# Expert inputs scattered to memory by row, and the second layer's expert results stored there

## The chip, the cores and the metric

The kernel runs on one core of one Trainium2 chip, in one launch. The metric is device microseconds of one execution; the median of three runs of the kernel before is 1235.07 us (1232.63 to 1237.51). Engines are called PE (matmuls), DVE, ACT and POOL (elementwise work), SP (it issues most DMAs). A DMA is issued on the queue of an engine; the data are moved by the core's 16 DMA engines.

## What is computed

Two layers, each a sequence mixer (convolution, mLSTM, gated linear recurrence) and a mixture of experts. Layer 1 of the experts (l = 0) runs on 512 tokens, 256 of them context; layer 2 (l = 1, `last` in the code) only on the 256 latent ones. Shapes here: 1024 model columns, 16 experts in 4 groups, two experts per token inside the best group, 512 columns inside an expert.

```python
def hier_moe(h, w_rg, b_rg, w_re, b_re, w_gate, w_up, w_down):
    hf = h.reshape(-1, shp[-1])
    ...
    combine = jnp.sum(jax.nn.one_hot(expert_id, N_EXPERTS) * top_w[..., None], axis=1)
    y = jnp.zeros(hf.shape, jnp.float32)
    for e in range(N_EXPERTS):
        ye = (jax.nn.silu(hf @ w_gate[e]) * (hf @ w_up[e])) @ w_down[e]
        y = y + combine[:, e:e + 1] * ye
    return y.astype(h.dtype).reshape(shp)

for l in range(DEPTH):
    ...
    v_lat = rms_norm(h_lat, norm2_g[l]) * (1 + mod_lat[4]) + mod_lat[3]
    h_lat = h_lat + mod_lat[5] * hier_moe(v_lat, *moe_p)
    if not last:
        ...
        h_ctx = h_ctx + mod_ctx[5] * hier_moe(v_ctx, *moe_p)
```

All is float32. The kernel computes each expert only for the tokens that chose it.

## The kernel before

A stage of the program follows another: mixer 0, the head of layer 1's experts, its 16 experts, mixer 1, head and experts of layer 2, the final norm.

**Head.** The router's choice gives for each token and expert a position in that expert's list (`pos`, `run`, `pm1`); lists have up to 128 places in the code that is concerned here, longer ones are done by `overflow`. The normed tokens vn are turned so that tokens lie on partitions, and split in a high and a low part (`vh`, `vl`) that can be multiplied exactly.

**An expert x** of the loop works in this order, on PE:
- `gu`: gate and up projections of the tokens in `XT` (transposed inputs of a pair of experts), for blocks of 32 or 64 tokens, each under a condition on the expert's count;
- the first turn of `gather` for the next pair `pr`: one-hot matrices P2 (from `onehot`, on DVE) times `vh` and `vl` bring the next pair's tokens, already transposed, into a bank that is copied to `XT`. Four turns make a pair, two in each expert; pair 0 is done in the head by `gather0`;
- `act`: transposes of the activations (8 in all) with silu and product on ACT and DVE;
- the second turn of `gather`;
- the down projection, and what becomes of its result.

**Results.** In layer 1 all experts but the last store their results by list place to Yd in memory (`store`, on ACT's queue); `fetch` gathers them by row for each token (indirect DMAs on POOL, row numbers `rowi`), `take` weights and adds them. In layer 2 every expert is "wide" (`pec`): `down_w`, then `prep` makes scaled one-hots PT, `spread_y` scales and splits, and `to_tokens` brings the result of the expert before to its tokens with matmuls, within the expert after. Yd is zeroed in mixer 0 by 15 stores of SP (line 873).

**Weights.** Each expert has six tiles of 1 MB: gate and up in two halves each, down in two. `ahead` issues them on SP into a ring of slots, 12 in layer 1 and 15 in layer 2, as fast as slots come free; slot names are tags of buffers that are shared with other tiles (`hl`, `uTa`, `uTb`, `B`, the `q4` buffers). `slots` lists them; the seventh load of layer 1, the second expert's first gate half, goes to "hl".

**Order.** PE's order is the one written in the code (a manual schedule); the orders of the other engines are made by a scheduler. DMAs that SP and ACT issue share eight semaphores in rotation (DMAHW0 to 7), so that the n-th waits for the (n−8)-th to have landed; POOL's have eight of their own (DMASW0 to 7).

Of the kernel before, what the change touches and what calls it, by code (L numbers as in the profile page):

```python
# [14 lines left out]
P = 128  # L15
# [11 lines left out]
OVER = 3  # L27
NPE = 1
# [11 lines left out]
def hybrid_kernel(ctx, tc, x, c, cx, c_ctx, w_mod, b_mod, norm1_g, norm2_g, w_in, conv_w, conv_b, conv_ln_g,  # L40
# [15 lines left out]
    Yd = dram.tile([NE - NPE, P, D], F32, name="Yd", tag="Yd")  # L56
    cnt = [0]
# [816 lines left out]


# [210 lines left out]
    def moe(l, hs, fill):  # L1086
# [4 lines left out]
        with tc.tile_pool(name=f"mo{l}", bufs=1, reuse_waits="tile") as mo, \  # L1091
                tc.tile_pool(name=f"op{l}", bufs=1, space=bass.MemoryType.PSUM, reuse_waits="tile") as ops:
            box["ps"], box["nps"] = ops, 4 if last else 6
            NB = {"t2": 3, "t4": 2, "q4": 6, "gr": NT // 2, "sm": 4, "t8": 2 if last else 1, "Y": 2 if last else 3, "Yp": 2}
            yp = "Yp" if last else "q4"

            pec = range(0 if last else NE - NPE, NE)
# [124 lines left out]
            def onehot(pr):  # L1222
                P2 = tmp.tile([P, NT, 256], F32R, "t4" if last else "q4", f"P2_{l}_{pr}")
                for j in range(2):
# [9 lines left out]
            def gather(pr, cp):  # L1234
                XT, P2 = st[pr]
# [37 lines left out]
            V.scalar_tensor_tensor(pm1, pos, 1.0, AA, op0=OP.add, op1=OP.mult)  # L1273
            onehot(0)
# [19 lines left out]
            V.tensor_copy(cnti, cntf)  # L1294

            V.tensor_tensor(m1[4], m1[3], m1[2], op=OP.subtract)
            S.activation(m1[4], m1[4], AF.Exp)
            V.tensor_scalar(m1[5], m1[4], 1.0, None, op0=OP.add)
            V.tensor_tensor(m1[5], m1[5], m1[1], op=OP.mult)
            w1 = m1[6]  # L1300
            V.reciprocal(w1, m1[5])
            w2 = m1[5]
            V.tensor_tensor(w2, w1, m1[4], op=OP.mult)
            spread(A1, oh1)
            spread(A2, oh2)
            A1, A2 = (a.rearrange("p i g j -> p i (g j)") for a in (A1, A2))
            Wt = mt("Wt", [P, NT, NE])
            wtmp = mt("wtmp", [P, NT, NE])
            V.tensor_tensor(Wt, A1, bc(w1, NE), op=OP.mult)
            V.tensor_tensor(wtmp, A2, bc(w2, NE), op=OP.mult)  # L1310
            V.tensor_tensor(Wt, Wt, wtmp, op=OP.add)
            if not last:
                fits = mt("fits", [P, NT, NE])
                V.tensor_scalar(fits, pos, float(P) - 0.5, None, op0=OP.is_lt)
                for x in pec:
                    V.memset(fits[:, :, ORDER[x]:ORDER[x] + 1], 0.0)
                row = mt("row", [P, NT, NE])
                V.tensor_tensor(row, pos, fits, op=OP.mult)
                V.tensor_tensor(row, row, ebase[:, None, :].to_broadcast([P, NT, NE]), op=OP.add)
                rowf = mt("rowf", [P, 2, NT])  # L1320
                rowi = mt("rowi", [P, 2, NT], I32)
                wsel = mt("wsel", [P, 2, NT])
# [6 lines left out]
                V.tensor_copy(rowi, rowf)  # L1329
            show(f"Wt{l}", Wt)  # L1330
# [6 lines left out]
            Z, X1 = [Y2], None  # L1337
            if last:
                X1 = ops.tile([P, 512], F32, name="X1", tag="X1")
                Z.append(ops.tile([P, 512], F32, name="Y3", tag="Y3"))  # L1340
# [19 lines left out]
            def by32(x, b):  # L1360
                return (last and b == 0) if x in pec else (not last and b == 1)
# [32 lines left out]
            def down(b, hT, ps, ws):  # L1394
                w, q = (64, 512) if b == 0 else (32, 256)
                o0 = 256 if b == 2 else 0
                for k in range(4):
                    if b == 0:
                        hk = hT[:, k, :]
                    else:  # L1400
                        hk = hT[:, 2 * (b - 1) + k % 2, 32 * (k // 2):32 * (k // 2) + 32]
# [7 lines left out]
            pend = []  # L1409

            def prep(x):
# [399 lines left out]
```

## Time and profile before

| | |
|---|---|
| median of the runs | 1235.07 us |
| profiled execution | 1238.83 us, span 1237.2 us |
| layer 1's experts on PE | 343.59 to 683.7 |
| layer 2's experts on PE | 947.93 to 1224.81 |
| PE busy | 1102.3 us, 89% |
| DVE, ACT, POOL busy | 634.5, 355.8, 184.4 us |
| DMA | 308.06 MB, mean 249 GB/s |

The span runs from the first to the last instruction of the profiled execution; that execution's own time is 1.6 us longer than its span. The shares are means over stages with different limits. A timeline row gives a start in us from the span's start, a duration, the engine, the line of the kernel, the operation with the tiles that it writes and reads, how many instructions stand in the row, and in brackets the idle time before it with what ended it. A window's row gives the busy time of each engine in a stretch, the clock granted to PE as a share of full speed, the DMA's share and its rate.

### The profile page before, as it was taken

How to read it: one execution, taken by the hardware profiler on the slowest of the kernel's cores; microseconds unless marked ns; L12 is line 12 of the kernel's file. 1: busy time of each engine (PE TensorE's matmuls, PEld its weight loads, DVE VectorE, ACT ScalarE, POOL GpSimd, SP SyncE). 2: the span in 40 equal slices, each digit the busy share in tenths (PEclk: the TensorE clock that was granted, in tenths of full speed). 3: DMA queues.
4: the chain of work that ended last, by engine and by line, in shares of the span. 5: the costliest groups of instructions: out<-in, count | busy, mean ns of one | idle time of the engine just before them, and what ended most of it. 6: DMA issues, size and time to landing. Idle time of an engine off the chain costs nothing. (4 is left out here: it accounts for less than half of the span.)

```text
span 1237.2 us, 21521 instructions
## 1 busy us (share of the span) xinstructions
PE 1102.3 (89%) x8703; PEld 757.8 (61%) x8703; DVE 634.5 (51%) x1411; ACT 355.8 (29%) x696; POOL 184.4 (15%) x143
## 2 busy tenths in 40 slices
PE   6999899999899899999898398989988989999997
PEld 4577688899655454545343166779876645656652
DVE  3879958841721111011101789945946655455553
ACT  3554254432311111111110353734533111111111
POOL 3412213322000000000000633102440000000000
PEclk9989999999999899999999798989898999999999
DMA  9635742575977777866776742345687998979940
GB/s 317 203 103 193 242 137 69 174 269 204 335 315 277 322 270 274 324 250 283 300 319 252 260 137 63 127 136 188 219 307 305 395 385 316 380 294 411 407 163 35
DMA packets 133956, 308.06 MB, mean 249 GB/s; under 512 B 15554, under 2 KB 98798, under 8 KB 113982
## 3 DMA queue, kind: packets, MB, share of 16 engines
q1 hardware_dynamic: 128896, 295.74, 64.6%
q10 hardware_dynamic: 3278, 5.55, 1.2%
q0 software_dynamic: 1648, 4.86, 1.0%
q8 instruction: 100, 1.64, 0.5%
q14 instruction: 34, 0.28, 0.1%
HBM read 296.16 MB, written 12.85 MB: 250 GB/s over the span
## 5 line engine op out<-in xcount | busy, mean ns | idle before, releaser
L1356 PE MATMUL ps<-w,XT 128*64 128x512 f32 x512 | 122.8, 612 | 18.9 <-DMA w<-in_w_up_dram 5.7
L1356 PE MATMUL X<-w,XT 128*32 128x256 f32 (+1 forms) x2016 | 132.0, 393 | 5.2 <-issue 3.1
L1356 PEld LDWEIGHTS X<-w,XT 128*32 128x32 f32 (+1 forms) x2016 | 77.2, 112 | 64.9 <-issue 33.4
L1391 DVE TENSOR_TENSOR hT<-sg,ps 128x256 f32<-128x256 f32 x48 | 19.3, 421 | 188.8 <-ACT sg L1382 188.6
L1356 PEld LDWEIGHTS ps<-w,XT 128*64 128x64 f32 x512 | 43.2, 141 | 94.6 <-issue 63.7
L1242 PE MATMUL ps<-P,vh 128*128 128x256 f32 x336 | 86.1, 293 | 1.7 <-PEq L1636 1.2
L1242 PE MATMUL ps<-P,vl 128*128 128x256 f32 x336 | 82.2, 281 | 0.0
L756 DVE SCALAR_TENSOR_TENSOR acc<-cb,cwh,acc 128x512 f32<-128x512 f32 (+1 forms) x120 | 80.2, 708 | 1.0
L1445 PE MATMUL Y<-w,hT 128*64 128x512 f32 x304 | 73.9, 607 | 1.6 <-DVE hT L1388 0.3
L1242 PEld LDWEIGHTS ps<-P,vh 128*128 128x128 f32 x336 | 63.8, 190 | 11.5 <-PEq L1636 6.2
L1242 PEld LDWEIGHTS ps<-P,vl 128*128 128x128 f32 x336 | 63.8, 190 | 0.5
L1571 POOL DMA_INDIRECT ya<-Yd,rowi x8 | 8.1, 1015 | 358.0 <-issue 358.0
L225 PE MATMUL ps<-w,cS 128*32 128x256 f32 x768 | 49.5, 396 | 9.9 <-DMA w<-in_w_mod_dram 9.6
L1403 PE MATMUL ps<-w,hT 128*64 128x512 f32 x240 | 54.8, 598 | 0.4 <-DVE hT L1391 0.3
L1489 DVE COPY Y<-Y 128x512 f32<-128x512 f32 x15 | 10.4, 692 | 84.8 <-DMA Yd<-Y 41.8
L1379 PE MATMUL ps<-blob,gs 128*128 128x128 f32 x256 | 41.1, 288 | 13.6 <-DVE gs L1368 3.7
L1373 ACT COPY gs<-ps 128x512 f32<-128x512 f32 x15 | 8.8, 586 | 146.0 <-PE ps L1356 107.0
L1445 PEld LDWEIGHTS Y<-w,hT 128*64 128x64 f32 x304 | 24.8, 139 | 34.9 <-issue 32.5
L191 ACT CAST y<-yt 128x512 fp32r<-128x512 f32 x30 | 18.1, 620 | 94.6 <-DVE yt L1461 94.6
L1379 PEld LDWEIGHTS ps<-blob,gs 128*128 128x128 f32 x256 | 27.5, 143 | 28.9 <-issue 12.9
L1246 ACT COPY XT<-ps 128x512 f32<-128x512 f32 x28 | 16.5, 590 | 88.9 <-PE ps L1242 88.5
L1382 ACT ACTIVATE sg<-ps 128x256 f32<-128x256 f32 x64 | 24.2, 388 | 61.9 <-PE ps L1379 61.7
(896 smaller groups left out, 2276.0 us busy)
## 6 DMA issues: line engine op xcount, KB each, us to landing
w<-in_w_down_dram SPq DMA_DIRECT2D x58, 1024.0 KB
w<-in_w_gate_dram SPq DMA_DIRECT2D x49, 1024.0 KB
w<-in_w_mod_dram SPq DMA_DIRECT2D x48, 1024.0 KB
w<-in_w_up_dram SPq DMA_DIRECT2D x48, 1024.0 KB
w<-in_w_in_dram SPq DMA_DIRECT2D x23, 1024.0 KB
w<-in_w_up_dram SPq DMA_DIRECT2D x32, 512.0 KB
w<-in_w_gate_dram SPq DMA_DIRECT2D x30, 512.0 KB
w<-in_w_out_dram SPq DMA_DIRECT2D x8, 1024.0 KB
```

The costliest lines, as they stand in the source:

```text
L191: S.copy(hi, raw)
L225: T.matmul(ps[32 * j:32 * j + 32, hf * 256:hf * 256 + 256], cS[:, k, :], w[:, k, :], start=(k < 4), stop=(k >= 4))
L756: V.scalar_tensor_tensor(acc[:, ch], src, wcol, acc[:, ch], op0=OP.mult, op1=OP.add)
L1242: T.matmul(ps[:, cc, :], v[:, i, k * P:k * P + P], P2[:, i, :], start=(n == 0), stop=(n == 2 * NT - 1))
L1246: S.copy(XT[:, 2 * cp:2 * cp + 2, :], ps)
L1356: T.matmul(ps[w * t:w * t + w, o0:o0 + q], XT[:, k, c0:c0 + w], ws[2 * g + k // 4][k % 4][:, f0:f0 + q], start=(k == 0), stop=(k == KC - 1))
L1379: T.transpose(pt[:, f, :], gs[:, f * P:f * P + P], ident)
L1382: S.activation(sg, pt[:, :, 0:64], AF.Silu)
L1391: V.tensor_tensor(hT, sg, pt[:, :, 64:128], op=OP.mult)
L1403: T.matmul(ps[w * t:w * t + w, o0:o0 + q], hk, ws[4 + k // 2][k % 2][:, q * t:q * t + q], start=(k == 0), stop=(k == 3))
L1445: T.matmul(Z[h][r0:r0 + 64, :], hT[:, k, :], ws[4 + k // 2][k % 2][:, 512 * h:512 * h + 512], start=(k == 0), stop=(k == 3))
L1489: V.tensor_copy(Y, ps)
```

## The change

Four things change.

1. **Inputs of pairs 1 to 7, both layers.** In the head, vn's rows are also copied unsplit (8 and 4 more copies), and indirect DMAs on POOL scatter them to a new tensor Xd in memory, at expert and list place (row numbers `rowx`; 8 scatters of 512 KB in layer 1, 4 in layer 2; in layer 1 the copies lie in the buffers "B" and "hl"). `xload`, on SP, reads a pair's rows back to the single buffer `xg`, which takes "uTb" from the slots (11 and 14 remain): the first 64 places of both experts, and the rest of each under a condition. `gather` is then 4 transposes a turn in place of 16 (layer 1) or 8 (layer 2) one-hot matmuls. Expert 0 has no turns, expert 1 has all four of pair 1, later experts two each. `onehot` remains for pair 0 and the last expert.
2. **Results of layer 2.** Experts 0 to 14 store to Yd as in layer 1, in blocks of 32 for the first 64 places; only the last expert remains wide. `fetch` and `take` are then used in layer 2 as well, at the last expert.
3. **Zeroing.** Xd is zeroed in mixer 0 by 16 stores on SP after Yd's.
4. The head computes `rowx` ahead of the weights of the tokens (`weights`).

```diff
@@ mixer 0 @@
                 for n in range(NE - NPE):
                     nc.sync.dma_start(Yd[n, 64:P, :], z[64 * (n % 2):64 * (n % 2) + 64, :])
+                for n in range(NE):
+                    nc.sync.dma_start(Xd[n], z)
             wvs = [wsplit(w_in[l], 1536 + 256 * hp) for hp in range(2)]
...
-            pec = range(0 if last else NE - NPE, NE)
+            pec = range(NE - NPE, NE)
...
             if last:
-                slots = ["B", "q4", "q4", "q4", "uLa", "uLb", *["r"] * RING, "uTa", "uTb"]
+                slots = ["B", "q4", "q4", "q4", "uLa", "uLb", *["r"] * RING, "uTa"]
             else:
-                slots = ["q4", "q4", *["r"] * 4, "hl", "uTa", "uTb", *["r"] * (RING - 4)]
+                slots = ["q4", "q4", *["r"] * 4, "hl", "uTa", *["r"] * (RING - 4)]
@@ gather @@
                 for cc in range(2):
                     k = 2 * cp + cc
-                    n = 0
-                    for i in range(NT):
-                        for v in (vh, vl):
-                            T.matmul(ps[:, cc, :], v[:, i, k * P:k * P + P], P2[:, i, :], start=(n == 0),
-                                     stop=(n == 2 * NT - 1))
-                            n += 1
+                    for j in range(2):
+                        T.transpose(ps[:, cc, j * P:j * P + P], xg[:, j, k * P:k * P + P], ident)
@@ head @@
+            if last:
+                vn2 = [tmp.tile([P, 2, D], F32, "t8", "vn1")]
...
+            if not last:
+                vn2 = [kt([P, 2, D], name=f"vn{t}", tag=t) for t in ("B", "hl")]
+            vn = [vn2[i // 2][:, i % 2] for i in range(NT)]
...
                     V.tensor_tensor(lo, src, hi.bitcast(F32), op=OP.subtract)
+                    o = vn[i][:, 512 * hf:512 * hf + 512].rearrange("t (k p) -> t k p", k=4)
+                    (S.copy, V.tensor_copy)[hf](o, src)
...
             gather0()
+            Xf = Xd.rearrange("e s d -> (e s) d")
+            for i in range(NT):
+                for cc in range(2):
+                    G.indirect_dma_start(out=Xf, out_offset=bass.IndirectOffsetOnAxis(ap=rowx[:, cc, i:i + 1], axis=0),
+                                         in_=vn[i], in_offset=None, bounds_check=NE * P - 1, oob_is_err=False)
+            xg = kt([P, 2, D], name=f"xg{l}", tag="uTb")
+            G.memset(xg[64:P], 0.0)
+            def xload(pr):
+                if pr < NE // 2:
+                    nc.sync.dma_start(xg[0:64], Xd[2 * pr:2 * pr + 2, 0:64, :].rearrange("e s d -> s e d"))
+                    for j in range(2):
+                        ...
+                        nc.sync.dma_start(xg[64:P, j], Xd[2 * pr + j, 64:P, :], cond=n_x > 64)
@@ expert loop @@
             ahead(0)
+            xload(1)
...
+                turns = ((), ()) if x == 0 else ((0, 1), (2, 3)) if x == 1 else ((2 * (x % 2),), (2 * (x % 2) + 1,))
...
-                if pend:
-                    to_tokens(*pend.pop(), totals())
                 if more:
-                    gather(pr, 2 * (x % 2))
+                    for cp in turns[0]:
+                        gather(pr, cp)
...
                 if more:
-                    gather(pr, 2 * (x % 2) + 1)
-                if last and x + 1 < NE:
-                    prep(x + 1)
+                    for cp in turns[1]:
+                        gather(pr, cp)
+                    if x % 2:
+                        xload(pr + 1)
...
+                elif last:
+                    down(0, hA, Y1, ws)
+                    with tc.If(n_e > 32):
+                        down(1, hA, Y1, ws)
+                    store(x, 0, Y1, n_s)
+                    with tc.If(n_e > 64):
+                        down(None, hB, Y2, ws)
+                    store(x, 1, Y2, n_s)
```

What this does to the order of three queues follows. `w` with a number is a weight tile, `DMAHW`, `DMASW` the DMA semaphores that a row waits for, an engine's name the wait for work of that engine.

SP before, where the experts of layer 1 are first loaded (w67 and w68 are expert 0's down, w69 to w74 all of expert 1, w75 to w80 of expert 2):

```order
L1128 DMA w67_3469<-in_w_down_dram 128x2048 [waits DMAHW7_49,PE_49]
L1128 DMA w68_3471<-in_w_down_dram 128x2048 [waits DMAHW0_49,PE_49]
L1128 DMA w69_3473<-in_w_gate_dram 128x2048
L1128 DMA w70_3475<-in_w_up_dram 128x2048 [waits DVE_49,PE_49]
L1128 DMA w71_3477<-in_w_gate_dram 128x2048 [waits DVE_49,PE_49]
...
L1122 DMA w75_3705<-in_w_gate_dram 128x1024 [waits DMAHW4_49,DVE_49,PE_49]
```

SP after, the same place and what follows, with the read-back of pair 1:

```order
L1134 DMA w67_3531<-in_w_down_dram 128x2048 [waits DMAHW7_49,PE_49]
L1134 DMA w68_3533<-in_w_down_dram 128x2048 [waits DMAHW0_49,PE_49]
L1134 DMA w71_3539<-in_w_gate_dram 128x2048 [waits DMAHW1_49,PE_49]
...
L1134 DMA w79_3757<-in_w_down_dram 128x2048 [waits DMAHW4_49,PE_49]
L1128 DMA w85_3990<-in_w_down_dram 128x1024 [waits DMAHW5_49]
...
L1134 DMA w69_3535<-in_w_gate_dram 128x2048 [waits DMASW2_49,DMASW1_49,DMASW7_49,DMASW0_49,DMAHW7_49,DVE_49,Activation_49]
L1335 DMA xg0_3485<-Xd_64 64x2x1024 [waits DMAHW0_49]
```

The load of w69 has moved from the third place of these to behind expert 2's loads, and waits for four of POOL's DMA semaphores; `xload(1)` stands directly behind it.

POOL before, at the head of layer 1's experts, up to the overflow's branches in expert 3 (branches left out):

```order
L270 TENSOR_TENSOR sq01_2937<-sq01_2937,mhalf_66 128x2 [waits DVE_49]
L270 TENSOR_TENSOR sq00_2995<-sq00_2995,mhalf_66 128x2 [waits DVE_49]
L759 MEMSET wr1_8494 128x256 [waits PE_49]
...
L1497 TENSOR_LOAD cnti0_3417 [waits DVE_49]
L1498 COMPARE_AND_BRANCH
```

POOL after, at the same place:

```order
L762 MEMSET wr1_8327 128x256 [waits PE_49]
L1330 MEMSET xg0_3485 64x2048 [waits DVE_49,PE_49,Pool_49]
L1327 DMA Xd_64<-vnB_3306,rowx0_3382 2048x1024 [waits DMASW3_49,DMAHW6_49,DVE_49,Activation_49]
L1327 DMA Xd_64<-vnB_3306,rowx0_3382 2048x1024 [waits DMASW4_49,DMASW3_49]
...
L1327 DMA Xd_64<-vnhl_3307,rowx0_3382 2048x1024 [waits DMASW1_49,DMASW0_49,Activation_49]
L1327 DMA Xd_64<-vnhl_3307,rowx0_3382 2048x1024 [waits DMASW2_49,DMASW1_49]
```

Eight scatters have come (four of them left out here), each of which waits for a semaphore that the one before it sets; four in layer 2 are chained alike.

SP in mixer 0, before:

```order
L187 DMA w_1066<-in_w_in_dram 128x8x256
L873 DMA Yd<-zero_1197 64x1024 x8
L187 DMA w_1214<-in_w_in_dram 128x8x256
L187 DMA w_1222<-in_w_in_dram 128x8x256
L187 DMA w_1454<-in_w_mod_dram 128x8x256
```

and after:

```order
L190 DMA w_1067<-in_w_in_dram 128x8x256
L876 DMA Yd<-zero_1198 64x1024 x8
L879 DMA Xd<-zero_1198 128x1024 x16
L190 DMA w_1231<-in_w_in_dram 128x8x256
L190 DMA w_1239<-in_w_in_dram 128x8x256
```

The 16 stores of zeros stand between Yd's and the next two weight loads, those of `wvs`.

## Rows read from the trace of the kernel before

**Rows 1.** The page: busy us (share of the span) and instructions of each engine; DMA total.
```profile
PE 1102.3 (89%) x8703; PEld 757.8 (61%) x8703; DVE 634.5 (51%) x1411; ACT 355.8 (29%) x696; POOL 184.4 (15%) x143
...
DMA packets 133956, 308.06 MB, mean 249 GB/s; under 512 B 15554, under 2 KB 98798, under 8 KB 113982
```

**Rows 2.** Timeline of PE, one layer-1 expert: start, us, line, operation, count [idle before].
```profile
382.74 7.09 PE L1356 MATMUL ps<-w,XT 128*64 128x512 f32 x32 [0.65 <-PEq L1674]
389.98 0.35 PE L1242 MATMUL ps<-P,vh 128*128 128x256 f32 x1
...
391.82 0.28 PE L1242 MATMUL ps<-P,vl 128*128 128x256 f32 x1
392.25 1.27 PE L1379 MATMUL ps<-blob,gs 128*128 128x128 f32 x8
...
399.31 1.08 PE L1356 MATMUL ps<-w,XT 128*64 128x512 f32 x4 [0.31 <-PEq L1672]
```

**Rows 3.** Timeline of PE, layer-1 expert 14, and the start of expert 15.
```profile
641.25 7.09 PE L1356 MATMUL ps<-w,XT 128*64 128x512 f32 x32 [0.56 <-PEq L1674]
649.12 1.27 PE L1379 MATMUL ps<-blob,gs 128*128 128x128 f32 x8 [0.78 <-PEq L1649]
...
654.64 1.04 PE L1356 MATMUL ps<-w,XT 128*64 128x512 f32 x2 [0.31 <-PEq L1672]
```

**Rows 4.** Windows: both layers' experts, a full DMA stretch, layer 2's end.
```profile
core 0: us, PE busy (x) PEld busy (x) DVE busy (x) ACT busy (x) POOL busy (x), PEclk, DMA share, GB/s
360.39:683.70 323.31, 297.39 (x2111) 151.53 (x2111) 42.52 (x105) 43.11 (x90) 3.95 (x4) 0.98 0.74 291
948.00:1188.00 240.00, 222.42 (x2323) 142.24 (x2326) 130.32 (x262) 38.71 (x74) 0.65 (x1) 0.99 0.90 359
1110.00:1170.00 60.00, 56.47 (x597) 37.35 (x590) 36.71 (x72) 10.21 (x20) 0.00 (x0) 1.00 1.01 410
1190.00:1225.00 35.00, 33.04 (x259) 15.56 (x257) 12.28 (x25) 2.75 (x6) 0.00 (x0) 0.95 0.01 1
```

**Rows 5.** DMA issues: KB each and median us to landing; window 680:682.5, then whole.
```profile
ya<-Yd,rowi POOLq DMA_INDIRECT x3, 5.8
...
ya<-Yd,rowi POOLq DMA_INDIRECT x8, 8.5
...
rows<-in_conv_w_dram POOLq DMA_DIRECT2D x1, 62.0 KB, 5.0
```

**Rows 6.** Timelines of SP, then DVE, at the head of layer 1's experts.
```profile
325.34 0.42 SPq L1128 DMA_DIRECT2D w<-in_w_gate_dram  x1
...
335.12 3.67 DVE L1287 TENSOR_TENSOR vl<-ps,vh 128x512 fp32r<-128x512 f32 x6
...
343.52 0.16 DVE L1329 CAST rowi<-rowf 128x8 int32<-128x8 f32 x1
```

**Rows 7.** Timelines of SP, ACT and DVE in mixer 0.
```profile
132.44 1.51 SPq L187 DMA_DIRECT2D w<-in_w_in_dram  x2
...
141.28 1.04 ACT L191 CAST w28h<-w 128x1024 fp32r<-128x1024 f32 x1
...
154.31 1.22 DVE L192 TENSOR_TENSOR w28l<-w,w28h 128x1024 fp32r<-128x1024 f32 x1
```

**Rows 8.** Timeline of PE: a layer-2 expert with few tokens, and the last one.
```profile
962.31 3.66 PE L1356 MATMUL X<-w,XT 128*32 128x256 f32 x64 [0.16 <-PEq L1664]
...
972.84 3.65 PE L1445 MATMUL Y<-w,hT 128*64 128x512 f32 x16
976.65 4.73 PE L1356 MATMUL X<-w,XT 128*32 128x256 f32 x82
...
1199.90 7.11 PE L1356 MATMUL X<-w,XT 128*32 128x256 f32 x128
1206.94 2.12 PE L1478 MATMUL ps<-y,PT 128*128 128x512 f32 x8
...
1217.72 7.09 PE L1445 MATMUL Y<-w,hT 128*64 128x512 f32 x32
```

More of the change, by code (lines that the diff above doesn't have):

```diff
@@ L27 @@
 OVER = 3
+NOROW = 65536.0
 NPE = 1
@@ L1222, in onehot @@
             def onehot(pr):
-                P2 = tmp.tile([P, NT, 256], F32R, "t4" if last else "q4", f"P2_{l}_{pr}")
-                for j in range(2):
+                P2 = None
+                js = {0: (0, 1), NE // 2 - 1: (1,)}.get(pr, ())
+                if js:
+                    P2 = tmp.tile([P, NT, 256], F32R, "t4" if last else "q4", f"P2_{l}_{pr}")
+                for j in js:
                     e = ORDER[2 * pr + j]
@@ L1294, in moe, with weights @@
             V.tensor_copy(cnti, cntf)
[L1296 to L1314, printed above, removed]
+            def weights():
+                V.tensor_tensor(m1[4], m1[3], m1[2], op=OP.subtract)
+                S.activation(m1[4], m1[4], AF.Exp)
+                V.tensor_scalar(m1[5], m1[4], 1.0, None, op0=OP.add)
+                V.tensor_tensor(m1[5], m1[5], m1[1], op=OP.mult)
+                w1 = m1[6]
+                V.reciprocal(w1, m1[5])
+                w2 = m1[5]
+                V.tensor_tensor(w2, w1, m1[4], op=OP.mult)
+                V.tensor_tensor(Wt, A1, bc(w1, NE), op=OP.mult)
+                V.tensor_tensor(wtmp, A2, bc(w2, NE), op=OP.mult)
+                V.tensor_tensor(Wt, Wt, wtmp, op=OP.add)
                 for x in pec:
                     V.memset(fits[:, :, ORDER[x]:ORDER[x] + 1], 0.0)
[L1317 to L1322, printed above, removed]
+                V.tensor_tensor(row, row, fits, op=OP.mult)
                 V.tensor_tensor(fits, fits, Wt, op=OP.mult)
@@ L1329, in moe @@
                 V.tensor_copy(rowi, rowf)
+            Wt = mt("Wt", [P, NT, NE])
+            rowi = mt("rowi", [P, 2, NT], I32)
+            wsel = mt("wsel", [P, 2, NT])
+            weights()
             show(f"Wt{l}", Wt)
@@ L1360, in by32 @@
             def by32(x, b):
-                return (last and b == 0) if x in pec else (not last and b == 1)
+                return last and b == 0 if last or x in pec else b == 1
             def evac(x, b, ps):
@@ L1408, in moe @@
             pt_ = {}
-            pend = []
             def prep(x):
@@ L1615, in moe @@
                                          max_val=NTOK)
-                elif not last:
-                    if x == pec[0]:
-                        fetch()
-                    if x == NE - 1:
+                else:
+                    fetch()
+                    if not last:
                         box["w0"] = [wsplit(w_in[1], a) for a in (0, 256)]
-                    Z[1:] = [bank()]
-                    V.memset(Z[1], 0.0)
+                        Z[1:] = [bank()]
+                        V.memset(Z[1], 0.0)
                 pa = X1 or bank()
-                if wide and last:
+                if last:
                     gu(x, 0, pa, ws)
-                    if x == 0:
+                    if wide:
                         prep(x)
@@ L1678, in moe @@
                 if x == OVER:
-                    if last:
-                        to_tokens(*pend.pop(), totals())
-                    else:
-                        gr = gate_rows(l, 5, mo, "gr", (0, 1), NT // 2)
+                    gr = gate_rows(l, 5, mo, "gr", range(NT // 2), NT // 2)
                     overflow()
@@ L1779, in _constants @@
     a[:, C_IOTA:C_IOTA + 128] = t + 1
-    for x in range(NE - NPE):
+    for x in range(NE):
         a[:, C_MISC + ORDER[x]] = 128 * x
```

113 lines of the change are left out of this document (57 added, 56 removed).

## The prediction

> **What bounds the kernel now.** I read the page first. TensorE (PE) is busy 89% of the span and the 16 DMA engines move 249 GB/s on average [rows 1]; such a mean hides stages, so I then read a table of windows. In layer 1's experts (from the second expert's start at 360.39 to 683.70) PE is busy 297.39 of 323.31 us and the DMA moves 291 GB/s; in layer 2's experts (948 to 1188) it moves 359, at a share of 0.90, and where it is full (1110 to 1170, share 1.01) 410, which I take as its ceiling [rows 4]. After 1190 there are no loads left, and PE still works until 1225 [rows 4]: it had fallen behind. So PE sets the end of both stages, with the DMA close behind it in layer 2. The timeline of PE then tells what an expert is made of [rows 2, 3].
>
> **What goes from PE in layer 1.** An expert with up to 64 tokens takes 399.31 − 382.74 = 16.57 us: gate and up 7.09, two turns of 16 gather matmuls, 8 transposes of its activations, down. One turn runs from 389.98 to 391.82 + 0.28, 2.1 us (the rows between are 14 of the same kind) [rows 2]. Seven pairs times four turns make 28 turns, 59 us; E0's two run before 360.39, so 26 turns, 55 us, lie behind it. In their place stand 16 transposes per pair. Eight transposes take 1.27 us [rows 2], so 16 take 2.5, at most 18 us for seven pairs. But the turns also covered waits: expert 14, which gathers nothing, takes 654.64 − 641.25 = 13.39 us and shows an idle 0.78 ahead of its transposes that the others don't [rows 3]. That is 3.2 less than 16.57. With its share of the transposes, partly in those gaps, an expert comes to about 14.0, so 2.5 us less on 13 experts: **−33 us**, not 55 − 18 = −37.
>
> **What the scatters add in layer 1.** In the new order each scatter on POOL waits for the semaphore of the one before it: eight in a chain. And the load of the second expert's first gate half (w69) goes to the slot that now holds half of the scatters' source; it waits for the last of them. Before it was issued at 325.34, before the experts began [rows 6]. Queued behind it on SP are pair 1's read-back and all further loads; PE has nothing to do between expert 0 and expert 1 but wait. The chain starts when the row numbers are there: the nearest row, the cast of rowi, is at 343.52 [rows 6], so about 345. The trace holds no scatter. The nearest row is the gather of the same size by row, 5.8 us from issue to landing with the DMA busy; over all eight of them it is 8.5; the shortest queue of POOL's that the trace shows, for 62 KB, is 5.0 [rows 5]. I take 5.8, since few of the loads are in flight beside this chain: 8 x 5.8 = 46 us, bounds 40 and 68. It ends at 391; w69 lands some 6 us later (one more link of the same kind, behind little else), so expert 1 starts at about 397 instead of 360.39: **+37 us**, from +31 to +59.
> The Trainium skill, DMA: Bandwidth & Descriptors (section Anatomy of one DMA — SWDGE (gpsimd) path), puts such a DMA at about 2.0 us plus its bytes over 436 GB/s. By it an estimate for 512 KB is 3.2 us and for the chain 26, and the sum would be 20 us less. The rows' 5.0 for 62 KB speaks against it in this kernel; no run shows a scatter yet.
>
> **Loads in layer 1.** Of PE's 323.31 us 26 are idle [rows 4]; I take them for waits on weights. From 397 on 78 of the 96 tiles are still to come, 82 MB, and about 11 MB of read-backs, stores and fetches: 93 MB. With 290 us for it that is 320 GB/s, above the 291 of before and below the ceiling of 410 [rows 4]. So it fits, but with one slot fewer (11 for 12) and the single buffer xg, whose read-back waits on SP for the last transposes of the pair before, with the loads queued behind it. I add **+8 us** (0 to 15) to the waits of before. Layer 1 in sum: +37 − 33 + 8 = +12.
>
> **Mixer 0.** 16 zero stores of 512 KB, 8.4 MB, stand on SP ahead of two weight loads issued at 132.44 [rows 7]. At the ceiling of 410 they take 20 us. The loads were cast at 141.28, but the low half of the first was made only at 154.31, behind other work on DVE [rows 7], and the matmuls that use it follow. 141.28 + 20 + 1.04 (the cast) = 162 against 154.31: up to 8 us later, less where the loads had landed well ahead of the cast, more by a few where the zeros don't reach the ceiling. **+6 us** (0 to 12).
>
> **Head.** Each head copies vn too: half the copies on DVE behind vl's, eight and four in all. One vl subtraction of that size is 3.67 / 6 = 0.6 us [rows 6]; the four on DVE in layer 1 are 2.4, half of it ahead of the gather of pair 0. **+1 us** for both layers.
>
> **Layer 2.** PE loses much here. An expert with up to 32 tokens runs from 962.31 to 976.65, 14.3 us [rows 8]. Of that go 2.1 for the spreading of the results of the expert before (2.12 in the last one), two gather turns of half the length (2.1, with 1.2 for the transposes that come), about 1 for the scaled one-hots and half of the 3.65 of down: it falls to about 8.5 us. Its six tiles are 6.3 MB, 15 us at 410. So PE's gain is nearly all lost: the DMA becomes the bound. The weights of 948 to 1188 are 240 us x 359 = 86 MB; the change adds 4 scatters, 7 read-backs, 15 experts' stores and 4 fetches, 11 MB by their sizes. 97 MB at 410 is 237 us: without any idle the last load lands at 1185, with the tenth of idle that the stage has now (24 us) at 1209. In the new order SP also waits for the four scatters (4 x 5.8 = 23 us) before it goes on past pair 1's read-back. Behind the last load, the second half of down, there remain most of the last expert's 24.9 us (1199.90 to 1217.72 + 7.09), less 2.12 for spreading and 5 for gate and up having landed two tiles earlier: 18 [rows 8]. 1209 + 18 = 1227 against 1224.8; with a few us of waits between stores on ACT and loads on SP, which share eight semaphores in rotation, **+4 us**, from −18 (no idle) to +12. What follows, the last adding to tokens and the output, stays.
>
> **Sum.** 12 + 6 + 1 + 4 = +23 us. The profiled execution took 1238.83 us with a span of 1237.2, 3.8 above the median of 1235.07; the difference is put on the median: 1258.
>
> **The rivals.**
> A, the forecast: 1258. Chance 0.56, spread from 1238 to 1280 by the bounds above.
> B, faster: the chain goes at 5.0 a link and the loads keep near 410. Then expert 1 starts 31 us late, the 33 us of gathers go, and half of the 26 us of weight waits goes too, since no one-hot buffer of a pair blocks the shared buffers any more: −15 in layer 1. In layer 2 the idle tenth fills: −18; mixer +2, head +1: −30, **1205**. For it: PE lost 33 and more in both layers and the ceiling leaves room in layer 1. Against: the stage mean has never been near 410 while slots turned over. It decides if the DMA's share is above 0.95 in layer 2 from its start. Chance 0.18.
> C, read-backs stall PE in layer 1: xg is issued in the middle of an odd expert and its first transposes come some 12 us later (down 3.7, gate and up 7.1, the turn). If eight tiles stand ahead of it in the DMA queue, 8.4 MB at 410 is 20 us, so 8 us too late, seven times 56; some 16 of that is in A's waits already: +40, **1298**. For it: one buffer only. Against: the weights ahead of it mostly wait for slots and are issued behind it. Chance 0.13.
> D, nothing to measure: the link of 5.8 holds waiting in full queues. Its bytes at 410 GB/s are 1.3 us, the least a link can be; halfway from there to 5.8 a link is 3.6, the chain 29 and not 46, expert 1 starts 17 us earlier, and layer 2 comes out even: 23 − 17 − 4 = +2, **1237**. For it: the DMA has little to move while the chain runs. Against: 5.0 for 62 KB. The rule of the Trainium skill quoted above (same page and section) gives nearly this. Chance 0.13.
>
> **How the numbers follow.** A measurement of this kernel tells about 0.5% (6 us) from no change. Faster: B and a little of A, 0.20. Same: most of D and A's lower edge, 0.16. Slower: the rest of A, and C, 0.64. The range from 1210 to 1298 leaves out half of B, half of C and the tails.
>
> **What would show it.** The scatters' issues on POOL, 5.8 us apart from about 345; a gap on PE before expert 1 of some 40 us, ended by the load of w69; experts of about 14 us in layer 1 and none of 16.6; in layer 2 a DMA share near 1 while PE waits for weights, and the end of loads only some 18 us ahead of PE's end, where 37 lay. In mixer 0 the first use of the two loads about 6 us late. I am wrong if the gap before expert 1 is under 25 us, if PE waits for xg in every pair, or if the loads of layer 2 end before 1195 less the shift of what came before.

## The result and the profile after

The changed kernel takes 1363.63 us (median, 1360.52 to 1365.68) against 1233.85 for the kernel before, measured with it: a ratio of 1.1045, interval 1.1008 to 1.1081. The forecast was 1258, with a range to 1298: the direction was right, but the time lies outside the range, and the loss, 130 us, is more than five times the 23 forecast. The profiled execution has a span of 1358.6 us, 121.4 longer than the span before. Lines of the changed kernel are a little further down than in the listing above: `gu` is L1402, `gather` L1250, the weight loads L1128 and L1134, the read-back L1335 and L1340.

The page's busy times and its DMA total, to lay beside [rows 1]:

```profile
PE 1034.5 (76%) x8207; PEld 685.4 (50%) x8207; DVE 531.6 (39%) x1181; ACT 369.3 (27%) x719; POOL 211.7 (16%) x165
...
DMA packets 144357, 337.41 MB, mean 248 GB/s; under 512 B 16548, under 2 KB 102352, under 8 KB 124640
```

PE does 68 us less and idles 189 us more; 29 MB more are moved at the same mean rate. The stages, read from PE's timeline (first and last matmul of each, us):

| stage | before | after | difference | forecast |
|---|---|---|---|---|
| mixer 0 and head, to expert 0's gate | 343.6 | 351.9 | +8.3 | +7 |
| layer 1: expert 0's gate to expert 1's gate | 16.8 | 54.3 | +37.5 | +37 |
| layer 1: expert 1's gate to the last down | 323.4 | 350.4 | +27.0 | −25 |
| mixer 1 and head | 264.2 | 265.3 | +1.1 | 0 |
| layer 2's experts | 276.9 | 321.2 | +44.3 | +4 |
| final norm and output | 12.4 | 15.5 | +3.1 | 0 |

Two rows of the table hold nearly all of the error: layer 1 after expert 1's start, 52 us, and layer 2, 40 us. The windows of these two stretches, to lay beside [rows 4], and of the kernel before the whole of layer 2; the last three columns are the granted clock, the DMA's share and its GB/s:

```profile
406.20:756.60 350.40, 279.93 (x1807) 116.82 (x1807) 36.03 (x70) 45.48 (x91) 7.21 (x8) 0.92 0.75 276
1021.90:1343.10 321.20, 205.66 (x2433) 122.41 (x2432) 43.40 (x88) 50.16 (x98) 11.84 (x11) 0.81 0.83 306
...
947.90:1224.80 276.90, 257.24 (x2593) 158.90 (x2592) 143.46 (x287) 41.46 (x80) 0.65 (x1) 0.98 0.79 313
```

In layer 1 the DMA is 0.75 busy and moves 276 GB/s, where it was 0.74 busy and moved 291 before. In layer 2 it is 0.83 busy at 306; over the whole stage it was 0.79 and 313 before (the 0.90 and 359 of [rows 4] leave out the end of the stage, which has no loads). So the DMA is not at its ceiling, and PE, idle for 70 us in layer 1 and 116 in layer 2, isn't busy either: both wait. What for, the views of waits tell (us in total, times, longest; SPq is SP's DMA queue): SP's in layer 1 from expert 1 on, in layer 2, and of the kernel before in layer 1:

```profile
SPq L1134 <- DMA Yd<-Y: 102.1, 10, 15.5
SPq L1128 <- DMA Yd<-Y: 32.0, 5, 15.0
SPq L1340 <- DMA Yd<-Y: 31.2, 2, 16.8
...
SPq L1134 <- DMA Yd<-Y: 73.6, 9, 13.9
...
SPq L1128 <- DMA Yd<-Y: 29.4, 5, 12.3
...
SPq L1128 <- DMA Yd<-Y: 80.8, 5, 18.0
SPq L1122 <- DMA Yd<-Y: 63.0, 5, 17.6
```

A load or read-back on SP waits here for a store of results, Yd<-Y, that ACT has issued: 165 us in layer 1, 103 in layer 2 (where the kernel before had no such stores), 144 in layer 1 before. One such wait in layer 2, with the timelines of ACT, SP and PE and windows of 4 us:

```profile
1214.30 1.77 ACTq L1518 DMA_DIRECT2D Yd<-Y  x3
...
1212.12 0.33 SPq L1134 DMA_DIRECT2D w<-in_w_gate_dram  x1
1226.37 0.33 SPq L1134 DMA_DIRECT2D w<-in_w_up_dram  x1
1226.79 0.66 SPq L1335 DMA_DIRECT2D xg<-Xd  x1
...
1217.08 1.92 PE L1402 MATMUL X<-w,XT 128*32 128x256 f32 x28 [0.61 <-DMA w<-in_w_up_dram]
1234.34 1.08 PE L1250 MATMUL ps<-blob,xg 128*128 128x128 f32 x4 [15.33 <-DMA xg<-Xd]
...
1216.00:1220.00 4.00, 2.40 (x36) 0.91 (x28) 0.00 (x0) 0.59 (x1) 0.00 (x0) 1.00 1.01 409
1220.00:1224.00 4.00, 0.00 (x0) 0.00 (x0) 0.00 (x0) 0.00 (x0) 0.00 (x0) 0.91 0.77 320
1224.00:1228.00 4.00, 0.00 (x0) 0.00 (x0) 0.00 (x0) 0.00 (x0) 0.00 (x0) 0.50 0.32 63
```

ACT stores an expert's results at 1214.30. SP's next load, of w_up, has its place in the rotation of eight semaphores behind that store, and is issued only when it has landed, at 1226.37; the read-back stands behind that. Meanwhile the DMA runs dry (63 GB/s in 1224 to 1228), PE waits 15.33 us for xg, and its granted clock, 0.91 in 1220 to 1224, is 0.50 in the next window, the lower of its two levels, 1.2 GHz; PE has been idle since 1219. Then the next expert begins the same round. PE's longest waits over the whole program are the read-backs and the load behind the chain of scatters:

```profile
PE ps L1250 <- DMA xg<-Xd: 101.2, 16, 15.5
PE ps L1402 <- DMA w<-in_w_gate_dram: 41.4, 3, 37.6
```

The chain of scatters took about the time that was forecast. POOL's, SP's and PE's timelines; then the DMA issues with their median us to landing, in layer 1 for the scatters from "B" and from "hl", and in layer 2:

```profile
351.82 1.13 POOL L1327 DMA_INDIRECT Xd<-vnB,rowx  x1 [6.91 <-DVE XT L1269]
359.84 0.99 POOL L1327 DMA_INDIRECT Xd<-vnB,rowx  x1 [6.88 <-DMA Xd<-vnB,rowx]
...
385.23 0.96 POOL L1327 DMA_INDIRECT Xd<-vnhl,rowx  x1 [6.74 <-issue]
...
396.97 0.97 POOL L1327 DMA_INDIRECT Xd<-vnhl,rowx  x1 [2.61 <-DMA Xd<-vnhl,rowx]
...
400.83 0.33 SPq L1134 DMA_DIRECT2D w<-in_w_gate_dram  x1
...
406.22 9.39 PE L1402 MATMUL ps<-w,XT 128*64 128x512 f32 x32 [37.60 <-DMA w<-in_w_gate_dram]
```

```profile
Xd<-vnB,rowx POOLq DMA_INDIRECT x4, 6.9
...
Xd<-vnhl,rowx POOLq DMA_INDIRECT x4, 3.5
...
Xd<-vn,rowx POOLq DMA_INDIRECT x4, 3.3
```

From the first issue at 351.82 to the last landing at 400.6 are 48.8 us, forecast 46. The first four links run beside weight loads and land after 6.9 us, the last four in a DMA with little else to do after 3.5. By the Trainium skill, DMA: Bandwidth & Descriptors (section Anatomy of one DMA — SWDGE (gpsimd) path), such a DMA takes about 2.0 us plus its bytes over 436 GB/s, an estimate of 3.2 us for 512 KB. The trace agrees with it (medians of 3.3 and 3.5) where few loads are under way and not where they are (6.9).

In mixer 0, SP's and PE's timelines:

```profile
132.19 19.23 SPq L879 DMA_DIRECT2D Xd<-zero  x16
151.52 2.74 SPq L190 DMA_DIRECT2D w<-in_w_in_dram  x2
...
161.30 1.22 PE L520 MATMUL ps<-w28h,uh0a 128*128 128x256 f32 x4 [9.78 <-ACT w28h L194]
```

The zeros hold SP until 151.52, 19 us later than the loads were issued before [rows 7], and PE waits 9.78 us for the cast of what the loads bring.

### The profile page after: what moved, and what is told of

It reads as the page before. It is cut to its first block, busy times and chain, and to the rows that moved or that the text cites. A ratio compares the mean times of both kernels' runs of the same rounds, so it can differ in the third digit from the quotient of the medians.

```text
span 1358.6 us, 20751 instructions
## 1 busy us (share of the span) xinstructions
PE 1034.5 (76%) x8207; PEld 685.4 (50%) x8207; DVE 531.6 (39%) x1181; ACT 369.3 (27%) x719; POOL 211.7 (16%) x165
## 5 line engine op out<-in xcount | busy, mean ns | idle before, releaser
L1402 PE MATMUL ps<-w,XT 128*64 128x512 f32 x512 | 132.1, 629 | 65.6 <-DMA w<-in_w_gate_dram 41.4
L1402 PE MATMUL X<-w,XT 128*32 128x256 f32 (+1 forms) x2016 | 138.9, 401 | 17.4 <-PEq L1700 6.5
L1250 PE MATMUL ps<-blob,xg 128*128 128x128 f32 x224 | 44.8, 332 | 102.4 <-DMA xg<-Xd 101.2
L1402 PEld LDWEIGHTS X<-w,XT 128*32 128x32 f32 (+1 forms) x2016 | 80.2, 114 | 76.2 <-issue 35.4
L1402 PEld LDWEIGHTS ps<-w,XT 128*64 128x64 f32 x512 | 41.3, 143 | 153.1 <-issue 108.4
L1250 PEld LDWEIGHTS ps<-blob,xg 128*128 128x128 f32 x224 | 32.3, 171 | 117.7 <-issue 98.0
L1514 DVE COPY Y<-Y 128x512 f32<-128x512 f32 x30 | 20.7, 691 | 140.4 <-PEq L1700 38.5
L1419 ACT COPY gs<-X 128x512 f32<-128x512 f32 x45 | 26.3, 589 | 175.3 <-PEq L1674 57.4
L1450 PE MATMUL Y<-w,hT 128*32 128x256 f32 (+1 forms) x912 | 63.9, 420 | 7.1 <-DMA w<-in_w_down_dram 4.6
L1425 PE MATMUL ps<-blob,gs 128*128 128x128 f32 x256 | 48.3, 331 | 26.7 <-ACT gs L1419 18.3
L1450 PEld LDWEIGHTS Y<-w,hT 128*32 128x32 f32 (+1 forms) x912 | 29.8, 119 | 38.8 <-issue 18.5
L1254 DVE COPY XT<-ps 128x512 f32<-128x512 f32 x28 | 19.2, 687 | 68.7 <-PE ps L1250 68.6
L1450 PEld LDWEIGHTS ps<-w,hT 128*64 128x64 f32 x240 | 17.0, 148 | 40.0 <-issue 30.1
```

The source lines that it names most:

```text
L1250: T.transpose(ps[:, cc, j * P:j * P + P], xg[:, j, k * P:k * P + P], ident)
L1254: V.tensor_copy(XT[:, 2 * cp:2 * cp + 2, :], ps)
L1402: T.matmul(ps[w * t:w * t + w, o0:o0 + q], XT[:, k, c0:c0 + w], ws[2 * g + k // 4][k % 4][:, f0:f0 + q], start=(k == 0), stop=(k == KC - 1))
L1419: S.copy(o, src)
L1425: T.transpose(pt[:, f, :], gs[:, f * P:f * P + P], ident)
L1450: T.matmul(ps[w * t:w * t + w, o0:o0 + q], hk, ws[4 + k // 2][k % 2][:, q * t:q * t + q], start=(k == 0), stop=(k == 3))
```

## The experiments

**Theories.** *Bytes*: the DMA is the bound, time follows the bytes (the forecast's view of layer 2). *Read-back*: read-backs stand in SP's queue behind loads and stall PE (rival C). *Ring*: the stores of results in the semaphore rotation (this rotation is what is called the ring from here on) keep the loads from running ahead. *Slot*, its rival in the expectations from e5 on: the loads wait for slots that PE frees, and the waits for stores only lie on top. They give different times when one thing is moved at a time.

**e1, results only.** All gathers stay one-hot in both layers; no scatter, no xg, no zeros of Xd. The edit of `gather`; the rest is taken away in the same way.

```diff
-                        T.transpose(ps[:, cc, j * P:j * P + P], xg[:, j, k * P:k * P + P], ident)
+                        for i in range(NT):
+                            for v in (vh, vl):
+                                T.matmul(ps[:, cc, :], v[:, i, k * P:k * P + P], P2[:, i, :], ...)
...
```

> Layer 2's results go through memory as in the changed kernel, but both layers gather by one-hot matmuls as before (no scatter, no read-back, no zeroing of Xd, the slot uTb given back). Read-back theory (the changed kernel loses its time on read-backs that stand in SP's queue and share semaphores with the stores, and on the chain of scatters): both are gone, layer 1 is as before (E1 starts near 360, layer ends near 684), layer 2 is shorter than before by some 10 us because PE does less and only the DMA limits; 1220 to 1232 us. Bytes theory (the DMA is the bound, time follows the bytes): 5 MB more than before in layer 2 is 12 us, so 1240 to 1250. If the stores alone hold up the loads through the shared semaphores: over 1255.

1249.82 us, ratio 1.0136 (1.0099 to 1.0173). Layer 1 is as before (339.9 against 340.2 us), layer 2 takes 283.5 us against 276.9, though PE does far less there (220 us busy against 257). So the stores alone cost more than they save. The time lies where Bytes put it (1240 to 1250); what parts Bytes from Ring is e5.

**e2, read-backs on POOL's queue.**

```diff
-                    nc.sync.dma_start(xg[0:64], Xd[2 * pr:2 * pr + 2, 0:64, :].rearrange("e s d -> s e d"))
+                    nc.gpsimd.dma_start(xg[0:64], Xd[2 * pr:2 * pr + 2, 0:64, :].rearrange("e s d -> s e d"))
...
```

> The changed kernel with the read-backs issued on POOL's queue instead of SP's, same bytes, same single buffer. Read-back theory: the read-back no longer stands behind weight loads nor waits for the landing of the stores of results; PE's waits for xg (about 101 us in the changed kernel, 80 of them in layer 2) fall below 40 and the time to 1290 to 1320. Bytes theory: same bytes, so 1350 to 1365. The chain before expert 1 (a gap of 37.6 us) stays in both.

1359.95 us, ratio 1.102 (1.0967 to 1.1074): no gain. PE's waits:

```profile
PE ps L1402 <- DMA w<-in_w_gate_dram: 47.3, 6, 38.4
PE X L1402 <- DMA w<-in_w_up_dram: 38.8, 21, 4.8
...
PE ps L1250 <- DMA xg<-Xd: 19.6, 3, 17.7
```

The wait for xg falls from 101.2 to 19.6 as expected, and waits for weights take its place. So the read-back theory falls as it was stated: the read-back was only what came last; the loads were late anyway. This time, too, lies where Bytes put it.

**e3, no slot "hl".** Layer 1 has 10 slots, and no load waits for the scatters.

```diff
-                slots = ["q4", "q4", *["r"] * 4, "hl", "uTa", *["r"] * (RING - 4)]
+                slots = ["q4", "q4", *["r"] * 4, "uTa", *["r"] * (RING - 4)]
```

> The changed kernel with the slot hl taken out of layer 1's ring (10 slots instead of 11), so that no weight load waits for the scatters. Chain theory: expert 1's first gate half loads early, its gate and up run right after expert 0, and only its gather turns wait for the chain of eight scatters; the gap of 37.6 us before expert 1 goes, a gap of some 25 to 30 us comes before its first transposes of xg; net gain 8 to 15 us, less what one slot fewer costs: 1345 to 1360. If the gap was not due to that load: the gap stays, 1363 to 1375.

1355.96 us, ratio 1.0984 (1.0943 to 1.1026). PE's timeline:

```profile
371.89 7.09 PE L1402 MATMUL ps<-w,XT 128*64 128x512 f32 x32 [0.31 <-PEq L1707]
...
409.79 0.45 PE L1250 MATMUL ps<-blob,xg 128*128 128x128 f32 x1 [27.23 <-DMA xg<-Xd]
```

Expert 1's gate comes at 371.9 instead of 406.2, its first transposes of xg at 409.8 instead of 419.1; the layer ends no earlier (760.2). The gap was due to that load, but it wasn't what the layer's end hung on.

**e4, scatter in layer 1 only.** Layer 2 gathers by one-hot, as in e1.

> Scatter and read-back in layer 1 only; layer 2 gathers by one-hot and has its results through memory. Read-back theory: layer 1 as in the changed kernel (E1 near 406, end near 757), layer 2 loses its 80 us of waits for xg and takes about 265 to 275 us instead of 321: 1305 to 1320. Bytes theory: only 6 MB go, 15 us: about 1348.

1323.85 us, ratio 1.0705 (1.0668 to 1.0743): between what Read-back and Bytes gave. Layer 2's scatter costs 40 us of the changed kernel, layer 1's 74 (against e1).

**e5, stores on POOL's queue.** The direct test of the ring; the same bytes, the same loads.

```diff
-                    nc.scalar.dma_start(Yd[x, s0:s0 + w, :].rearrange("s (h f) -> h s f", f=q), Y[:, q * c:q * c + q],
+                    nc.gpsimd.dma_start(Yd[x, s0:s0 + w, :].rearrange("s (h f) -> h s f", f=q), Y[:, q * c:q * c + q],
```

> The changed kernel with the stores of results (Yd) issued on POOL's queue instead of ACT's, so that they leave the rotation of eight semaphores that the weight loads go through; same bytes. Ring theory (a weight load waits for the landing of the store issued eight DMAs earlier, which itself waits for an expert's end, so the loads can't run ahead): SP's 268 us of waits for Yd go, 1270 to 1310 us, with the 38 us gap of the scatter chain left. Slot theory (the loads wait for slots that PE frees, the stores' waits only lie on top): 1345 to 1365. Bytes theory: 1355 to 1365.

1278.78 us, ratio 1.0338 (1.0321 to 1.0355), as Ring gave it: 85 us less by the queue of the stores alone, with the same slots. In SP's waits none for results in Yd is left. So neither the bytes nor the slots were the bound for these 85 us. The move also takes the issue of the stores from ACT: PE's waits for ACT's copies (gs) fall from 18.3 to 8.1 us. So some 10 of the 85 may be that, which no run parts from the ring.

**e6, e1 with the stores on POOL.**

> e1 (results of layer 2 through memory, all gathers by one-hot) with the stores on POOL's queue. Ring theory: e1's 275 us of waits of SP for Yd go and with them PE's waits for w_up and w_gate in layer 2; 1200 to 1222, faster than both kernels. Slot theory or bytes theory: as e1, 1243 to 1255.

1192.49 us, ratio 0.9641 (0.9623 to 0.9659): faster than both kernels, and by more than Ring gave.

**e7, the kernel before with the stores on POOL.**

> The kernel before with layer 1's stores on POOL's queue. Ring theory: the ring held up loads there too (SP waited 165 us for Yd), but PE was idle for only 26 us in layer 1, so at most that can go: 1212 to 1228. Slot theory: no change, 1230 to 1238.

1210.31 us, ratio 0.9785 (0.9769 to 0.9802), a little less than Ring gave. Layer 1 from expert 1 on, to lay beside the 323.31 us of [rows 4]:

```profile
359.50:666.70 307.20, 289.92 (x2111) 151.45 (x2111) 46.54 (x110) 47.42 (x94) 27.26 (x54) 0.99 0.83 313
```

The ring was there before; it cost 16 us in layer 1 (324.0 against 340.2) and 8 in mixer 1 (256.6 against 264.2). So storing layer 2's results (e6 against e7) is worth 18 us where the stores don't hold up the loads, and cost 14 (e1) where they do.

**e8, stores and read-backs on POOL, no slot "hl".**

> The changed kernel with stores and read-backs on POOL's queue and without the slot hl: three couplings taken away at once. Ring theory: 1235 to 1275, of which 25 to 30 us are the chain of scatters before the first read-back and 8 us the zeroing. Slot theory: above 1330, since one slot fewer is left.

1259.76 us, ratio 1.018 (1.0161 to 1.0199). Still 67 us behind e6. Windows of e5 and of e6, for layer 1 from expert 1 on and for layer 2:

```profile
407.80:703.40 295.60, 263.07 (x1807) 113.67 (x1807) 38.15 (x73) 45.53 (x91) 26.48 (x51) 0.97 0.93 330
964.20:1260.90 296.70, 199.56 (x2433) 117.44 (x2432) 43.34 (x88) 49.91 (x97) 27.24 (x56) 0.84 0.91 332
...
359.70:666.90 307.20, 290.43 (x2111) 151.47 (x2111) 47.85 (x110) 47.41 (x94) 28.44 (x55) 0.99 0.84 316
923.70:1173.70 250.00, 207.70 (x2545) 124.95 (x2544) 46.45 (x105) 48.89 (x97) 23.22 (x52) 0.95 0.92 367
```

In layer 1 the transposes leave PE with 263 us of work in e5, the gathers with 290 in e6; yet the stretch is only 11.6 us shorter. The DMA is 0.93 busy in e5 and moves 330 GB/s with it, where e6 moves 316 with 0.84. In layer 2, 0.91 busy brings 332 GB/s, in e6 0.92 brings 367. So with read-backs a busy DMA seems to move less; these are means over whole stages, and e13 tests it.

**e9 and e10, the chain hidden, the zeros late.** Pair 1 is gathered by one-hot matmuls too, so that the scatters have until pair 2. In the expectations from here on, Read-back means that reading back costs DMA time. e10 also issues the zeros behind the two loads.

```diff
-            xload(1)
+            xload(2)
...
-                js = {0: (0, 1), NE // 2 - 1: (1,)}.get(pr, ())
+                js = {0: (0, 1), 1: (0, 1), NE // 2 - 1: (1,)}.get(pr, ())
...
-                    if x % 2:
+                    if x % 2 and pr > 1:
```

> e8 (stores and read-backs on POOL, no slot hl) with pair 1 gathered by one-hot matmuls in experts 0 and 1, in both layers, so that the chain of scatters has until pair 2. Chain theory: the gaps before the first transposes of xg in e8 (30.9 us in layer 1, 21.5 in layer 2) go and with them 40 to 50 us: 1208 to 1220. Read-back theory (in e8 the DMA was busy 0.90 to 0.95 at only 340 GB/s, so reading back costs DMA time and the loads used the gaps): 15 to 30 us go, 1230 to 1245.

> e9 with the 16 stores of zeros to Xd issued after the two weight loads that they stood in front of in mixer 0. If the 8 us that the first experts start later in the changed kernel come from these stores: 5 to 8 us less than e9. If from the head's extra copies: 0 to 2 us less.

1250.89 us, ratio 1.0136 (1.0103 to 1.0169), and 1243.8, ratio 1.0067 (1.0047 to 1.0087). Hiding the chain brings 9 us by the medians (5 by the ratios, whose intervals overlap), though PE waited over 50 for it in e8; both theories gave more. That the loads run ahead while PE waits is my reading, without a run for it; e9 also gives PE pair 1's one-hot matmuls back. The zeros' place is worth 7 (expert 0's gate at 347.2 instead of 352.5); 3.6 us of the later start remain, which I put down to the head's copies without a run for it.

**e11 and e12, scatter in one layer only, all of that out of the way.** e11 in layer 1 with the zeros late, e12 in layer 2.

> Scatter in layer 1 only, with pair 1 by one-hot, zeros late, stores and read-backs on POOL, no slot hl; layer 2 gathers by one-hot. To compare with e6 (1192.5), which has no scatter. If taking the gather matmuls off PE pays once chain, stores and zeros are out of the way: layer 1 takes 300 us or less against 324 in e6, 1165 to 1178. Read-back theory: the DMA becomes the bound in layer 1 too, 315 to 330 us, 1185 to 1205.

> Scatter in layer 2 only, with pair 1 by one-hot, stores and read-backs on POOL; layer 1 gathers by one-hot. To compare with e6 (1192.5). Read-back theory: layer 2 is bound by the DMA in e6 already (0.92 busy, 367 GB/s), so PE's gain is worth nothing and the extra 7 MB cost 20 to 40 us beside the 5 to 8 of the zeros: 1215 to 1240. If only the chain hurt there: 1197 to 1205.

1210.65 us, ratio 0.9782 (0.9747 to 0.9817), and 1233.33, ratio 0.9982 (0.9967 to 0.9996). Both are slower than e6 with no scatter, by 18 and 41 us: e11 lies above the range that Read-back gave, e12 in its own. Of the 41 some 8 are the zeros, which stand early in e12 (expert 0's gate at 351.2 against 343.0 in e6); of the 18 some 4 are the later start (347.1). e11 in layer 1, and e12 in layer 2, to lay beside e6's above:

```profile
363.90:681.00 317.10, 265.61 (x1823) 119.90 (x1823) 37.20 (x72) 45.60 (x92) 38.38 (x76) 0.94 0.91 333
...
935.50:1219.80 284.30, 204.83 (x2449) 117.11 (x2448) 43.08 (x90) 49.84 (x97) 32.57 (x74) 0.89 0.91 344
```

In e11 PE's work is 25 us less than in e6, and the stretch is 10 us longer, with the DMA at 0.91 and 333 GB/s. In e12 it is 3 us less and the stretch 34 us longer.

**e13, e14, e17, e18, the pieces of it in layer 2 with PE's work as in e6.** The gathers stay one-hot, and what is moved besides isn't used: the read-backs alone (e13), the scatters alone (e14), the same reads from rows of w_down (e17), and nothing but the slot taken away that xg takes (e18). All read-backs are on POOL's queue. e17's edit, against e13:

```diff
-                    nc.gpsimd.dma_start(xg[0:64], Xd[2 * pr:2 * pr + 2, 0:64, :].rearrange("e s d -> s e d"))
+                    nc.gpsimd.dma_start(xg[0:64], w_down[l, 2 * pr:2 * pr + 2, 0:64, :].rearrange("e s d -> s e d"))
...
```

> e6 with layer 2's seven read-backs of Xd (zeros, never scattered to) done beside the one-hot gathers and not used; one slot fewer, zeros of Xd issued late. To compare with e6 (1192.5). If the read-back is dear by itself: 4.2 MB cost 20 us or more, 1212 to 1225. If it costs only its bytes at 410 GB/s: 10 us or less, 1195 to 1205.

> e6 with layer 2's four scatters (and the extra copies of vn) done beside the one-hot gathers and never read; no zeros. If only the read-back is dear: 2 MB at 410 GB/s, 5 us, 1194 to 1200. If the scatters hold up the loads: above 1205.

> e13 with the seven unused reads taken from rows of w_down instead of Xd, same shapes, same queue, no zeros. If any such reads beside the loads cost that: as e13, 1208 to 1215. If it is the reading of Xd: 1195 to 1203.

> e6 with one slot fewer for layer 2's weights (14 instead of 15), which the read-back buffer takes; nothing else. If the slot is part of e13's 20 us: 1197 or more; otherwise 1190 to 1195, as e6.

1212.55 (ratio 0.982, 0.9797 to 0.9843), 1193.12 (0.9651, 0.9625 to 0.9677), 1212.34 (0.9816, 0.98 to 0.9832) and 1192.25 us (0.9659, 0.9642 to 0.9676). Against e6's 1192.49 the scatters and the slot cost nothing that the runs can tell; reading 4 MB beside the loads costs 20 us, twice what they take at 410 GB/s, from either tensor. e13's windows, 40 us with read-backs and 40 after them, then its DMA queues in each (packets, MB, share; q1 carries SP's loads, q0 what POOL issues):

```profile
966.00:1006.00 40.00, 28.89 (x364) 19.15 (x359) 4.64 (x12) 6.63 (x14) 3.99 (x9) 0.87 1.02 343
1046.00:1086.00 40.00, 34.73 (x364) 19.51 (x358) 7.42 (x19) 7.59 (x17) 2.92 (x6) 0.96 1.02 411
...
q1 hardware_dynamic: 2015, 11.50, 82.3%
q0 software_dynamic: 1008, 2.10, 18.9%
...
q1 hardware_dynamic: 2584, 15.68, 96.0%
```

The DMA is full in both (1.02); with the read-backs it moves 343 GB/s, without them 411. The loads themselves are slowed: 11.50 MB in 82.3% of 40 us are 349 GB/s, 15.68 in 96.0% are 408. POOL's queue is not the reason. In e5 SP issues the read-backs, and a slow stretch of a full DMA follows each of layer 2's last five; two windows of 4 us from one of them, in which PE waits for xg:

```profile
1072.00:1076.00 4.00, 0.00 (x0) 0.00 (x0) 0.00 (x0) 0.00 (x0) 0.00 (x0) 0.50 1.03 226
1076.00:1080.00 4.00, 0.00 (x0) 0.00 (x0) 0.00 (x0) 0.00 (x0) 0.00 (x0) 0.50 1.03 197
```

**e15 and e16, another layout of xg.** The pair's experts lie in the lower and the upper 64 partitions, so that both halves are written. The edit against e12 and e11:

```diff
-                    nc.gpsimd.dma_start(xg[0:64], Xd[2 * pr:2 * pr + 2, 0:64, :].rearrange("e s d -> s e d"))
+                    for j in range(2):
+                        nc.gpsimd.dma_start(xg[64 * j:64 * j + 64, 0], Xd[2 * pr + j, 0:64, :])
...
```

> e12 (scatter in layer 2 only) with another layout of xg: the first 64 places of the pair's two experts lie in the lower and the upper 64 partitions, so that a read-back writes to all 128 partitions; same bytes, same number of transposes. Partition theory: its packets fall from about 330 ns to about 160 and the time by 8 to 20 us from 1233: 1213 to 1225. If the packets are slow for another reason: 1228 to 1238.

> e11 (scatter in layer 1 only, everything else out of the way) with the same layout of xg. Partition theory: 1190 to 1203 against 1210.7; otherwise 1207 to 1214.

1232.08 us (ratio 0.9981, 0.9961 to 1.0002; e12 0.9982) and 1206.31 (0.9782, 0.9745 to 0.9819; e11 0.9782). No difference: the partitions are not why the read-backs are dear. What is, stays open.

**The sum.** From the changed kernel down to e6, each by one step: stores off the ring −85, read-backs on POOL and no slot "hl" −19, chain hidden −9, zeros late −7, layer 2's scatter and read-back −33, layer 1's −18, together 171 us. The parts hold in this order only: taken out of the changed kernel first, layer 2's scatter and read-back were worth 40 us (e4), and read-backs on POOL (e2) and no slot "hl" (e3) 4 and 8.

## Why the prediction was wrong

**Chain, mixer 0, head: right in sum, in part by luck.** Chain 46 us forecast, 48.8 measured; expert 1 +37 and +37.5; mixer and head +7 and +8.3. The first links follow each other after 8 to 9 us, the last after 4, where the row of 5.8 [rows 5] was taken for all: the two errors cancel. Of the +8.3 the zeros' place is 5.3 (e10) and what remains 3.6, where +6 and +1 were forecast. What the chain cost the end is another matter: hiding it brought 9 us (e9).

**Gather matmuls: right on PE, wrong on the end.** 37 us less work for PE and 33 less of its path were forecast; its work in that stretch falls by 34, from 297.39 [rows 4] to 263.07 us in e5, where the clock is nearly the same (0.98 and 0.97). The stretch itself was 295.6 us in e5 and 350.4 in the changed kernel. That e5 is 28 us shorter than before, near the −25 forecast for the stage, is luck: 16 of it is the ring, which e7 takes away too, and the gathers bring the other 12.

**"Loads in layer 1: +8 us (0 to 15)": the step that failed, by 52 us.** With the −33 as forecast, this term measured +60. I compared 320 GB/s wanted with a ceiling of 410 and took the 26 us of idle PE as waits on weights that would stay; PE's waits in that stretch name weights for 8.6 of them. The rate was not set by the ceiling but by when SP may issue: with the stores off the rotation the stretch is 55 us shorter (e5). The rotation of eight semaphores stood in my text, priced at "a few us" in layer 2; in layer 1 not at all, though the waits of SP for Yd, 144 us there before, could have been read. They were for the most part hidden (e7: 16 us) beside a PE that needed 16.6 us an expert. With PE at 14 they set the pace, and PE, with more idle time, ran at a granted clock of 0.92 instead of 0.98: 280 us of busy time in place of 263.

**"Layer 2: +4": the same step, by 40 us.** The same ring, new in this layer and priced at "a few us", costs about 24 (321.2 against 296.7 us in e5). The rest is scatter and read-back, which 11 MB at 410 GB/s, 27 us, were to cover, with the idle tenth of the stage on top: a full DMA moved 343 beside read-backs, so that 4 MB alone cost 20 us (e13).

**The rivals.** C came nearest (1298), with half of the loss. Its sign came, PE waiting for xg 16 times (101.2 us), but 79.7 us of that in layer 2, where C had none, and it wasn't the mechanism: read-backs that no longer stood behind loads (e2) gave nothing. B's condition, the DMA above 0.95 from the start of layer 2, didn't come; e6 is faster than B's 1205, but by another way, without the scatters that B keeps. D's link of 3.6 came in the second half of the chain alone. The rule of the Trainium skill in the prediction would have shortened the chain by 20 us. The trace agrees with it for links without loads beside them (3.5) and not for the others (6.9).

## What to carry to other kernels

Ask of each DMA that a change adds which semaphores and which queue it shares with the loads, and read what the loading queue already waits for: a wait that is hidden beside a busy engine becomes the bound when that engine gets faster. A rate read in one stretch is a ceiling only for the same kind of transfers. Stores of results whose issue hangs on compute belong on a queue that no prefetch goes through: here that alone was worth 26 us before the change and 85 after it.

## What was not expected of the hardware

A DMA that is 1.02 busy moved 411 GB/s of weights alone and 343 with 512 KB read-backs among them (e13), with the same cost for reads of a weight tensor (e17), and no gain from a layout over all partitions (e15). The loads fell from 408 to 349 GB/s of their own share meanwhile, and with read-backs on SP's queue a full DMA moved 197 and 226 (e5). The cause is open. An indirect scatter of 512 KB landed in 3.5 us (median of four) in a quiet DMA and in 6.9 beside loads. After a wait of 37.6 us, 32 matmuls of gate and up took 9.39 us instead of 7.09, at a granted clock of 0.75 (406.2 to 415.6), so in part at 1.2 GHz.
